# The gate and up blocks of a feed-forward network: four quads in blocks 3 to 10, and two pairs a block with their low parts from an adding DMA

## Chip, cores and metric

The kernel runs on one core of a Trainium2 chip. The metric is the device time of one execution in microseconds (us), given as the median of several runs. Engines are named as in the profile: PE (TensorE, matrix products), DVE (VectorE), ACT (ScalarE), POOL (GpSimd), SP (SyncE, which issues loads).

## What is computed

One layer on 256 tokens of width 2048, in fp32: a SwiGLU network, a mixer (an RWKV7 scan, a pooling branch and an output projection) and a second SwiGLU network, each between two RMS norms and added to the residual. The change lies in the two SwiGLU networks:

```python
def _swiglu(x, w_gate, w_up, w_down):          # x: 256 x 2048, D_FF = 5632
    return (jax.nn.silu(x @ w_gate) * (x @ w_up)) @ w_down
...
    h = x
    f = _swiglu(_rmsnorm(h, ln_ffn1_pre[l]), ffn1_gate[l], ffn1_up[l], ffn1_down[l])
    h = h + MACARON_WEIGHT * _rmsnorm(f, ln_ffn1_post[l])
    mx = _hybrid_mixer(_rmsnorm(h, ln_mix_pre[l]), ...)
    h = h + _rmsnorm(mx, ln_mix_post[l])
    f = _swiglu(_rmsnorm(h, ln_ffn2_pre[l]), ffn2_gate[l], ffn2_up[l], ffn2_down[l])
    h = h + MACARON_WEIGHT * _rmsnorm(f, ln_ffn2_post[l])
```

## The kernel before

**Products.** PE multiplies in fp32r, a shorter form of fp32. So every operand is kept as a high part (rounded to fp32r) and a low part (what is left), and a product is three matmuls: high by high, low by high, high by low (`mm3`, L316 to L320). One matmul is 128 x 128 by 128 x 512. For every weight tile ACT makes the high part (a cast) and DVE the low part (the weight less the high part).

**Blocks.** The gate and up weights of a network are cut into 11 blocks of 512 columns (0 to 10). In a block the 2048 rows are 16 k-tiles of 128. A *pair* is two k-tiles of one weight for both token halves: one load of 128 x 1024, a cast (L372), a low (L382) and 12 matmuls (`fetch` L361, `pair` L538). A *quad* (`quad` L549) takes two k-tiles of gate and up together in a Strassen-like scheme: 7 products instead of 8, so 21 matmuls stand for the 24 of a gate pair and an up pair. It costs DVE three sums of weights (t13 at L570, t2 at L575, t4 at L579) and four lows (L592), and ACT four casts (L587). `seven` (L502) runs a block: after its last quad `merge` (L642, additions at L639) adds the quads' products up, then come Silu (L1061), the product of gate and up (L1068) and a transpose (L869). The carry (`carry`) moves the result with 16 small DMAs of POOL (L886) to the layout that the down product wants; ACT and DVE split it at L899 and L903.

**The order of a block** stands in a string of `GATE_UP` (L48): f is the next gate pair, l the next up pair, q the next quad. Quads take the first k-tiles, pairs the others. Block 1 is sixteen pairs; the others alternate:

```python
GATE_UP = ["", "ffffffffllllllll"] + ["fffqffqllqlll", "ffqfqfqlqlll"] * 4 + ["fffqffqllqlll"]
```

So blocks 2, 4, 6, 8, 10 have three quads and five gate and five up pairs (183 matmuls), blocks 3, 5, 7, 9 have four quads and four of each (180 matmuls). A capital F or L is a pair whose low part a DMA adds; no string has one.

**Buffers and order.** Weights land in w32 (4 buffers) or in general units of 128 x 1024; 33 units exist, and activations and the tiles of h hold more and more of them as blocks go by. High and low parts go to a ring of 5 (wH, wL), or to units (kH, kL). A planner (`Plan.solve`, L136) fixes the order on each engine from rough costs before the kernel is written: it follows the PE order, gives each step a due time, starts loads at most `FETCH` (22 us) ahead of it, and takes buffers as they come free. Loads are issued by SP, in order; SP waits until the target buffer is free, and what stands behind waits too. ACT, DVE and POOL also work their queues in order.

Of the kernel before, what the change touches and what calls it, by code (L numbers as in the profile page):

```python
# [23 lines left out]
W = 1024  # L24
# [22 lines left out]
OUT = ((0, "", 0), (1, "fffqfq" "qlqlll", 0), (3, "", TRAIL))  # L47
GATE_UP = ["", "ffffffffllllllll"] + ["fffqffqllqlll", "ffqfqfqlqlll"] * 4 + ["fffqffqllqlll"]  # L48
SUMS = (2, 2)
# [7 lines left out]
EARLY = 0.5  # L57
RATE, LEAVE, LAND, ADD, MOVE = 0.28, 1.05, 2.0, 10.0, 12.0

# [29 lines left out]
class Plan:  # L89
# [46 lines left out]
    def solve(s):  # L136
# [46 lines left out]
        while len(order) < len(s.nodes):  # L183
# [17 lines left out]
            if n.size:  # L201
                start = max(n.free + LEAVE, line)
                line = start + n.size / RATE
                n.end = max(n.end, (line if n.eng == "SP" else n.free + LEAVE + n.size / RATE)
                            + LAND)
            for k in n.rel:
# [13 lines left out]
class Block:  # L220
# [140 lines left out]
    def fetch(s, w, k, c0, keep, hold=False, by_dma=False):  # L361
# [29 lines left out]
        return p.op("DVE", cost("DVE", 1024), low, [n], rel=[src]), dst  # L391

    def halves_of(s, w32, hold=False):
        if hold:
            wH, wL = s.unit(dt=F32R, p="kH"), s.unit(dt=F32R, p="kL")
        else:
            wH = s.wp.tile([P, 1024], F32R, tag="wH", name=s.nm("wH"), bufs=WS_BUFS)
            wL = s.wp.tile([P, 1024], F32R, tag="wL", name=s.nm("wL"), bufs=WS_BUFS)
        return [t.rearrange("p (k c) -> p k c", k=2) for t in (w32, wH, wL)]
# [102 lines left out]
    def seven(s, wf, cf, wl, cl, at, dep, KT, need, sm, order, ev_f, ev_l, used, trail=0):  # L502
# [27 lines left out]
        def rows(k, h):  # L530
            xH, xL = at(k)
            return xH[:, h * P:h * P + P], xL[:, h * P:h * P + P]
# [5 lines left out]
        def pair(k, w, c0, b, by_dma):  # L538
            low, dst = s.fetch(w, k, c0, keep, by_dma, by_dma)

            def do():
                for i in range(2):
                    for h in range(2):
                        mul(f"{b}{h}", rows(k + i, h), ws[k + i])
            d = p.pe(12 * MM, do, [low, dep(k)] + claim(b + "0", b + "1"), dst)
            used.setdefault(k // 4, []).append(d)
            return d
# [105 lines left out]
        nq, last = 0, {}  # L653
        ks = dict(f=iter(range(K0, KT, 2)), l=iter(range(K0, KT - trail, 2)))
        for c in order:
# [9 lines left out]
            w_ = (wf, cf) if c == "f" else (wl, cl)  # L665
            last[c] = pair(next(ks[c]), *w_, c, by_dma)
            left[c] = left.get(c, 0) + 1
# [1338 lines left out]
```

## Time and profile before

| | |
|---|---|
| runs shown | 3: median 2019.09 us (2018.82 to 2020.29) |
| profiled execution | 2018.42 us, span of its instructions 2016.7 us |
| granted PE clock | 0.999 |
| busy in the span | PE 99%, DVE 90%, ACT 59%, POOL 16% |
| loads (queue q1) | 384.70 MB in 204649 packets |
| matmuls of 128 x 512 in the six largest groups | 3 x 2128 for pairs, 3 x 270 for quads |

A view by stretch gives each engine's busy time between two times. A view by group gives busy time, count and mean of one, and the idle time just before with what ended it. The timeline gives instructions by start. A busy PE means that matmuls are in flight, not that it runs at its peak.

### The profile page before, as it was taken

What the parts mean: (1) busy time and instruction counts of PE and PEld (TensorE: products, weight loads), DVE (VectorE), ACT (ScalarE), POOL (GpSimd) and SP (SyncE); (2) the same over time, 40 slices, a digit from 0 to 9 for tenths busy, and PEclk for the clock granted to TensorE, in tenths of its full rate; (3) what the DMA queues carried; (4) which work ended last, traced back from release to release, by engine and by line L of the source; (5) the groups of instructions that cost most, each with busy time, mean ns of one, the idle gap of its engine ahead of it and who ended that gap; (6) DMA issues with size and microseconds to landing.
All of it is one profiled execution on the core that took longest, in us unless ns stands there. A gap on an engine that the chain in (4) does not pass through costs nothing.

```text
span 2016.7 us, 28695 instructions
## 1 busy us (share of the span) xinstructions
PE 2002.8 (99%) x9963; PEld 1655.3 (82%) x9963; DVE 1821.7 (90%) x2418; ACT 1189.3 (59%) x1582; POOL 326.3 (16%) x673
## 2 busy tenths in 40 slices
PE   9999999999999999999999999999999999999997
PEld 7888888888888888888788788888888888888886
DVE  6999999999999957799689678979999999999997
ACT  7565665656666566685476435665566556556663
POOL 0111131131000123413220111011121211310000
PEclk9999999999999999999999999999999999999999
DMA  7775565676568677757456558667656656765683
GB/s 270 254 239 173 188 217 200 203 221 228 186 203 299 209 212 213 205 175 214 147 173 189 159 168 269 245 218 245 223 176 202 218 196 190 230 229 188 207 294 126
DMA packets 227355, 423.56 MB, mean 210 GB/s; under 512 B 24575, under 2 KB 28041, under 8 KB 227209
## 3 DMA queue, kind: packets, MB, share of 16 engines
q1 hardware_dynamic: 204649, 384.70, 59.2%
q0 software_dynamic: 22272, 36.51, 5.5%
q8 instruction: 78, 1.28, 0.3%
q10 hardware_dynamic: 288, 0.52, 0.1%
q14 instruction: 68, 0.56, 0.1%
HBM read 396.69 MB, written 8.39 MB: 201 GB/s over the span
## 4 chain that ended last, share of the span: by engine, by line
PE 97%; DVE 1%; issue 1%; DMA 0%; ACT 0%; POOLq 0%; POOL 0%; DVEq 0%; SPq 0%
PE mm L318 27%; PE mm L320 26%; PE mm L319 26%; PE ms L319 5%; PE ms L320 5%; PE ms L318 5%; PE tr L843 1%; PE pA L1724 0%; DVE u L639 0%; PE mc L811 0%; PE pU L1820 0%; PE pSa L1832 0%; DMA w<-in_ffn_gate_dram 0%; PE pY L1855 0%; PE pT L1891 0%
## 5 line engine op out<-in xcount | busy, mean ns | idle before, releaser
L318 PE MATMUL mm<-wH,xH 128*128 128x512 f32 (+1 forms) x2128 | 830.1, 391 | 0.0
L320 PE MATMUL mm<-wH,xL 128*128 128x512 f32 (+1 forms) x2128 | 825.8, 388 | 0.5 <-DVE xL L861 0.5
L319 PE MATMUL mm<-wL,xH 128*128 128x512 f32 (+1 forms) x2128 | 825.7, 388 | 0.0
L320 PEld LDWEIGHTS mm<-wH,xL 128*128 128x128 f32 x2128 | 399.4, 188 | 83.5 <-DVE xL L861 1.4
L318 PEld LDWEIGHTS mm<-wH,xH 128*128 128x128 f32 x2128 | 399.5, 188 | 82.5 <-ACT xH L852 0.2
L319 PEld LDWEIGHTS mm<-wL,xH 128*128 128x128 f32 x2128 | 399.7, 188 | 80.6
L372 ACT CAST wH<-w 128x1024 fp32r<-128x1024 f32 x317 | 330.7, 1054 | 224.8 <-PE mm L320 192.2
L382 DVE TENSOR_TENSOR wL<-w,wH 128x1024 fp32r<-128x1024 f32 x317 | 377.9, 1217 | 22.8 <-ACT wH L372 20.4
L587 ACT CAST wH<-t 128x1024 fp32r<-128x1024 f32 x204 | 215.1, 1055 | 226.2 <-PE mm L320 117.7
L295 DVE TENSOR_TENSOR wL<-w,wH 128x1024 fp32r<-128x1024 f32 (+2 forms) x200 | 236.5, 1191 | 94.9 <-ACT wH L294 93.3
L294 ACT CAST wH<-w 128x1024 fp32r<-128x1024 f32 (+2 forms) x200 | 205.3, 1034 | 171.0 <-PE mm L320 149.7
L886 POOL DMA_DIRECT2D x<-T x352 | 172.5, 497 | 730.5 <-DVE T L869 245.5
L592 DVE TENSOR_TENSOR wL<-t,wH 128x1024 fp32r<-128x1024 f32 x204 | 242.8, 1215 | 1.7 <-ACT wH L587 1.7
L587 ACT CAST wH<-w 128x1024 fp32r<-128x1024 f32 x204 | 165.6, 834 | 50.4 <-PE mm L320 30.8
L592 DVE TENSOR_TENSOR wL<-w,wH 128x1024 fp32r<-128x1024 f32 x204 | 191.2, 950 | 0.0
L570 DVE TENSOR_TENSOR t<-w,w 128x1024 f32<-128x1024 f32 x102 | 123.9, 1215 | 0.0
L319 PE MATMUL ms<-wL,sH 128*128 128x512 f32 x270 | 105.5, 391 | 0.2
L320 PE MATMUL ms<-wH,sL 128*128 128x512 f32 x270 | 105.1, 389 | 0.0
L318 PE MATMUL ms<-wH,sH 128*128 128x512 f32 x270 | 105.1, 389 | 0.0
L579 DVE TENSOR_TENSOR t<-w,t 128x512 f32<-128x512 f32 x102 | 70.3, 689 | 2.2
L575 DVE TENSOR_TENSOR t<-w,t 128x512 f32<-128x512 f32 x102 | 69.9, 686 | 1.1
L639 DVE TENSOR_TENSOR u<-ms,u 128x512 f32<-128x512 f32 x92 | 61.3, 685 | 1.4
(313 smaller groups left out, 2099.3 us busy)
## 6 DMA issues: line engine op xcount, KB each, us to landing
w<-in_w_in_dram SPq DMA_DIRECT2D x128, 512.0 KB
w<-in_ffn_up_dram SPq DMA_DIRECT2D x114, 512.0 KB
w<-in_ffn_gate_dram SPq DMA_DIRECT2D x112, 512.0 KB
w<-in_ffn_down_dram SPq DMA_DIRECT2D x104, 512.0 KB
w<-in_ffn_down_dram SPq DMA_DIRECT2D x144, 256.0 KB
w<-in_ffn_gate_dram SPq DMA_DIRECT2D x128, 256.0 KB
w<-in_ffn_up_dram SPq DMA_DIRECT2D x124, 256.0 KB
w<-in_w_out_dram SPq DMA_DIRECT2D x24, 512.0 KB
```

What stands on the lines that cost most here:

```text
L294: s.nc.scalar.copy(vH, v)
L295: s.nc.vector.tensor_tensor(out=vL, in0=v, in1=vH.bitcast(F32), op=ALU.subtract)
L318: nc.tensor.matmul(ps, aH, bH, start=start, stop=False)
L319: nc.tensor.matmul(ps, aH, bL, start=False, stop=False)
L320: nc.tensor.matmul(ps, aL, bH, start=False, stop=stop)
L372: nc.scalar.copy(x["H"], x["v"])
L382: nc.vector.tensor_tensor(out=x["L"], in0=x["v"], in1=x["H"].bitcast(F32), op=ALU.subtract)
L570: V.tensor_tensor(out=v["t13"], in0=v["a"], in1=v["b"][:, :1].to_broadcast([P, 2, 512]), op=ALU.subtract)
L579: V.tensor_tensor(out=v["t24"][:, 1], in0=v["b"][:, 1], in1=v["t24"][:, 0], op=ALU.subtract)
L587: nc.scalar.copy(H, src)
L592: V.tensor_tensor(out=L, in0=src, in1=H.bitcast(F32), op=ALU.subtract)
L886: nc.gpsimd.dma_start(out=x[0][q * 32:q * 32 + 32, i], in_=src[i * 32:i * 32 + 32, q])
```

## The change

Blocks 3 to 10 all get the string `ffqfqFqlqllL`: four quads, four gate pairs and four up pairs, 180 matmuls. Block 2 keeps three quads. The third gate pair (F) and the last up pair (L) are always k-tiles 14 and 15 (`KM`), and take a new way, `fetch_added`: the weight is loaded into a unit, ACT casts the high part (L404), ACT also writes the negated weight in fp32r (L408), and a DMA issued by POOL adds the weight to it, unit to unit in SBUF (L411). DVE has no part in it. Such a pair holds three units; the weight's is free when the add has landed. Its load stands outside the chain that orders the others and may start 28 us ahead (`FETCH + AHEAD`). The planner's time for an add goes from 10 to 8, and a DMA of POOL now counts in the line of transfers as those of SP do.

```diff
--- before.py
+++ after.py
@@ -45,7 +45,7 @@
 DOWN = ((0, "fffffffffffqfff" "qllqllqllqllqllqllqll", 0),
         (2, "fqflqfqflqfqflqfqflqfqfqff", TRAIL))
 OUT = ((0, "", 0), (1, "fffqfq" "qlqlll", 0), (3, "", TRAIL))
-GATE_UP = ["", "ffffffffllllllll"] + ["fffqffqllqlll", "ffqfqfqlqlll"] * 4 + ["fffqffqllqlll"]
+GATE_UP = ["", "ffffffffllllllll"] + ["fffqffqllqlll", "ffqfqFqlqllL", "ffqfqFqlqllL", "ffqfqFqlqllL", "ffqfqFqlqllL", "ffqfqFqlqllL", "ffqfqFqlqllL", "ffqfqFqlqllL", "ffqfqFqlqllL"]
 SUMS = (2, 2)
 BY_DMA = range(0)
 LAT = dict(PE=0.22, DVE=0.1, ACT=0.17, SP=0.0, POOL=8.0)
@@ -55,7 +55,8 @@
 SPARE, KEEP, URGENT, HOLD = 3, 4, 8.0, 99
 SOON, FETCH, LATEST, BEFORE = 22.0, 22.0, 12.0, 12.0
 EARLY = 0.5
-RATE, LEAVE, LAND, ADD, MOVE = 0.28, 1.05, 2.0, 10.0, 12.0
+AHEAD, MSPARE, KM = 6.0, 0, 14
+RATE, LEAVE, LAND, ADD, MOVE = 0.28, 1.05, 2.0, 8.0, 12.0
 
 ROWS = [("ln_mix_pre", 16), ("ln_ffn2_pre", 16), ("mu", 26), ("w0", 8), ("a0", 8),
         ("k_k", 8), ("k_a", 8)]
@@ -201,8 +202,7 @@
             if n.size:
                 start = max(n.free + LEAVE, line)
                 line = start + n.size / RATE
-                n.end = max(n.end, (line if n.eng == "SP" else n.free + LEAVE + n.size / RATE)
-                            + LAND)
+                n.end = max(n.end, line + LAND)
             for k in n.rel:
                 k.left -= 1
                 k.end = max(k.end, n.end)
@@ -390,6 +390,31 @@
             return p.op("POOL", 1.25, low, [n], size=0.94, lat=ADD), dst
         return p.op("DVE", cost("DVE", 1024), low, [n], rel=[src]), dst
 
+    def fetch_added(s, w, k, c0, keep):
+
+        nc, p, x = s.nc, s.plan, {}
+        dst = [Tok("unit"), Tok("unit"), Tok("unit")]
+        by_k = lambda t: t.rearrange("p (k c) -> p k c", k=2)
+
+        def load():
+            x["W"] = s.get_w(w, k, 2, c0, 512, own=dst[0].of == "unit")
+
+        def cast():
+            x["H"] = s.unit(dt=F32R, p="kH")
+            nc.scalar.copy(x["H"], x["W"])
+
+        def minus():
+            x["L"] = s.unit(dt=F32R, p="kL")
+            nc.scalar.activation(out=x["L"], in_=x["W"], func=AF.Copy, scale=-1.0)
+
+        def low():
+            nc.gpsimd.dma_start(out=x["L"], in_=x["W"], accum_op=ALU.add)
+            keep([(k + i, by_k(x["H"])[:, i], by_k(x["L"])[:, i]) for i in range(2)])
+        n = p.op("SP", 0.4, load, take=dst[:1], size=0.52, ahead=FETCH + AHEAD, spare=MSPARE)
+        h = p.op("ACT", cost("ACT", 1024), cast, [n], take=dst[1:2])
+        n = p.op("ACT", cost("ACT", 1024), minus, [n, h], take=dst[2:])
+        return p.op("POOL", 1.25, low, [n], size=0.94, lat=ADD, rel=dst[:1]), dst[1:]
+
     def halves_of(s, w32, hold=False):
         if hold:
             wH, wL = s.unit(dt=F32R, p="kH"), s.unit(dt=F32R, p="kL")
@@ -536,12 +561,14 @@
             ws.update((k, (wH, wL)) for k, wH, wL in tiles)
 
         def pair(k, w, c0, b, by_dma):
-            low, dst = s.fetch(w, k, c0, keep, by_dma, by_dma)
+            got = {}
+            low, dst = (s.fetch_added if by_dma else s.fetch)(
+                w, k, c0, lambda tiles: got.update((i, wt) for i, *wt in tiles))
 
             def do():
                 for i in range(2):
                     for h in range(2):
-                        mul(f"{b}{h}", rows(k + i, h), ws[k + i])
+                        mul(f"{b}{h}", rows(k + i, h), got[k + i])
             d = p.pe(12 * MM, do, [low, dep(k)] + claim(b + "0", b + "1"), dst)
             used.setdefault(k // 4, []).append(d)
             return d
@@ -651,7 +678,8 @@
                 held[b].append(d)
                 use[i][1].append(d)
         nq, last = 0, {}
-        ks = dict(f=iter(range(K0, KT, 2)), l=iter(range(K0, KT - trail, 2)))
+        ks = {c: iter([k for k in range(K0, k1, 2) if k != KM or c.upper() not in order])
+              for c, k1 in (("f", KT), ("l", KT - trail))}
         for c in order:
             if c == "q":
                 last["q"] = quad(nq)
@@ -663,7 +691,7 @@
                 continue
             by_dma, c = c in "FL", c.lower()
             w_ = (wf, cf) if c == "f" else (wl, cl)
-            last[c] = pair(next(ks[c]), *w_, c, by_dma)
+            last[c] = pair(KM if by_dma else next(ks[c]), *w_, c, by_dma)
             left[c] = left.get(c, 0) + 1
             if c == "f" and left["f"] == std // 2:
                 m["f"] = last["f"]
```

The lines below L205 move by up to 28: L570, L575, L579, L587 and L592 become L597, L602, L606, L614 and L619, L886 becomes L914, L899 becomes L927; L372 and L382 stay.

DVE, first network, block 4, around its second and third quads: t13 and t24 are sums of weights of one quad, wL from w32 at L382 is a pair's low, wL at L592 or L619 a quad's. Before:

```order
L570 TENSOR_TENSOR t13_523_2306<-w32_494_2166,w32_497_2177 128x1024
L575 TENSOR_TENSOR t24_526_2311<-w32_494_2166,t13_523_2306 128x512
L382 TENSOR_TENSOR wL_525_2309<-w32_478_2087,wH_524_2308 128x1024
L592 TENSOR_TENSOR wL_529_2318<-w32_481_2106,wH_528_2317 128x1024
L592 TENSOR_TENSOR wL_533_2330<-w32_482_2109,wH_532_2329 128x512
L579 TENSOR_TENSOR t24_526_2311<-w32_497_2177,t24_526_2311 128x512
L592 TENSOR_TENSOR wL_538_2344<-t13_513_2254,wH_537_2343 128x1024
L592 TENSOR_TENSOR wL_540_2361<-t24_521_2295,wH_539_2360 128x1024
L570 TENSOR_TENSOR t13_541_2371<-w32_509_2244,w32_510_2247 128x1024
L575 TENSOR_TENSOR t24_544_2376<-w32_509_2244,t13_541_2371 128x512
L382 TENSOR_TENSOR wL_543_2374<-w32_489_2146,wH_542_2373 128x1024
```

and now:

```order
L597 TENSOR_TENSOR t13_527_2312<-w32_502_2186,w32_503_2188 128x1024
L619 TENSOR_TENSOR wL_526_2310<-t24_519_2268,wH_525_2309 128x1024
L602 TENSOR_TENSOR t24_529_2322<-w32_502_2186,t13_527_2312 128x512
L606 TENSOR_TENSOR t24_529_2322<-w32_503_2188,t24_529_2322 128x512
L597 TENSOR_TENSOR t13_533_2330<-w32_507_2214,w32_509_2218 128x1024
L382 TENSOR_TENSOR wL_532_2328<-w32_501_2184,wH_531_2327 128x1024
L619 TENSOR_TENSOR wL_538_2345<-w32_502_2186,wH_537_2344 128x1024
L619 TENSOR_TENSOR wL_540_2349<-w32_503_2188,wH_539_2348 128x512
L602 TENSOR_TENSOR t24_547_2381<-w32_507_2214,t13_533_2330 128x512
L619 TENSOR_TENSOR wL_546_2365<-t13_527_2312,wH_545_2364 128x1024
L619 TENSOR_TENSOR wL_549_2384<-t24_529_2322,wH_548_2383 128x1024
L606 TENSOR_TENSOR t24_547_2381<-w32_509_2218,t24_547_2381 128x512
```

Where each quad had a pair's low behind it, two quads' sums now stand together with one pair's low.

ACT, the same block: wH is a tile of the ring, xH a tile of h, kH and kL are a pair's high part and negated weight in units. Before:

```order
L587 CAST wH_457_1982<-w32_410_1767 128x512
L587 CAST wH_459_1998<-t13_433_1893 128x1024
L587 CAST wH_463_2019<-t24_437_1912 128x1024
L899 CAST xH_465_2024<-x32_401_1734 128x4x128 x2
L372 CAST wH_469_2043<-w32_418_1818 128x1024
L372 CAST wH_471_2055<-w32_424_1842 128x1024
L587 CAST wH_473_2065<-w32_427_1865 128x1024
```

and now:

```order
L1089 ACTIVATE u_427_1854<-u_427_1854 128x512
L614 CAST wH_429_1875<-t13_413_1788 128x1024
L404 CAST kH_436_1905<-w32_423_1834 128x1024
L408 ACTIVATE kL_438_1910<-w32_423_1834 128x1024
L614 CAST wH_440_1926<-t24_432_1881 128x1024
L372 CAST wH_444_1940<-w32_398_1706 128x1024
L614 CAST wH_448_1950<-w32_404_1748 128x1024
```

The cast at L404 and the negated copy at L408 stand in a row among the ring's casts; kL_438 is the low part of block 4's up pair, which PE uses 130 matmuls after it first uses wH_440, the cast behind it.

POOL, first network, blocks 0 to 4: x32<-T1 are the carry's moves, kL<-w32 the adds. Before:

```order
L886 DMA x32_198_786<-T1_192_761 32x256 x16
L886 DMA x32_297_1270<-T1_294_1251 32x256 x16
L886 DMA x32_401_1734<-T1_391_1684 32x256 x16
L886 DMA x32_468_2030<-T1_462_2004 32x256 x16
L886 DMA x32_571_2497<-T1_559_2441 32x256 x16
```

and now:

```order
L914 DMA x32_198_786<-T1_192_761 32x256 x16
L914 DMA x32_298_1272<-T1_294_1251 32x256 x12
L411 DMA kL_311_1332<-w32_293_1249 128x1024
L914 DMA x32_298_1272<-T1_294_1251 32x256 x4
L411 DMA kL_352_1524<-w32_333_1443 128x1024
L411 DMA kL_392_1681<-w32_378_1624 128x1024
L914 DMA x32_401_1719<-T1_395_1695 32x256 x16
L411 DMA kL_438_1910<-w32_423_1834 128x1024
L411 DMA kL_478_2065<-w32_465_2010 128x1024
```

The adds stand between the moves of one block's carry and the next, the first of them inside one.

## The prediction

> **What bounds the kernel now.** I read the page first: busy times, then the chain that ended last.
>
> ```profile
> span 2016.7 us, 28695 instructions
> PE 2002.8 (99%) x9963; PEld 1655.3 (82%) x9963; DVE 1821.7 (90%) x2418; ACT 1189.3 (59%) x1582; POOL 326.3 (16%) x673
> PE 97%; DVE 1%; issue 1%; DMA 0%; ACT 0%; POOLq 0%; POOL 0%; DVEq 0%; SPq 0%
> ```
>
> PE is busy for 99% of the span and carries 97% of the chain. A busy PE need not be at its peak, so I looked next at the changed place alone: busy time by stretch, one stretch for each gate/up block. Counting 192 + 192 + 183 matmuls for blocks 0 to 2 puts block 3 of the first FFN at 140.34 us. Columns: length, then busy time and count of each engine, granted clock, DMA share, GB/s.
>
> ```profile
> core 0: us, PE busy (x) PEld busy (x) DVE busy (x) ACT busy (x) POOL busy (x), PEclk, DMA share, GB/s
> 140.34:181.14 40.80, 40.80 (x182) 33.78 (x180) 40.56 (x47) 25.23 (x28) 7.82 (x16) 1.00 0.68 230
> 181.14:222.62 41.48, 41.48 (x185) 34.35 (x183) 41.27 (x50) 24.73 (x29) 7.81 (x16) 1.00 0.60 198
> 387.25:428.20 40.95, 40.95 (x182) 33.70 (x180) 40.71 (x48) 23.93 (x26) 7.82 (x16) 1.00 0.69 210
> 428.20:469.68 41.48, 41.48 (x185) 34.35 (x183) 40.83 (x47) 24.36 (x27) 7.83 (x16) 1.00 0.74 229
> 140.34:469.68 329.34, 329.34 (x1454) 272.43 (x1452) 326.26 (x374) 196.62 (x220) 62.62 (x128) 1.00 0.64 208
> 1448.78:1778.10 329.32, 329.32 (x1453) 272.44 (x1452) 326.23 (x374) 196.58 (x220) 62.61 (x128) 1.00 0.64 208
> ```
>
> The first row is block 3 (four quads), the second block 4 (three quads). 40.80 us for 180 weight loads, one for each matmul, and 41.48 us for 183 are both 0.2267 us for one matmul, at full clock. 1452 x 0.2267 is 329.1, so in blocks 3 to 10 PE loses about 0.2 us an FFN. PE is the limit and its work is what must shrink. But DVE stands right behind: 326.26 of 329.34 us, idle 0.24 and 0.21 us in the first two rows. Both engines have to be followed.
>
> **PE's part of the change.** A quad is 21 matmuls in place of the 24 of a gate pair and an up pair. Blocks 4, 6, 8 and 10 go from three quads to four, in both FFNs: 8 quads, 24 matmuls less, which is also the difference between the two PE orders. 24 x 0.2267 = **5.44 us less**. As PE is never idle there, this is a gain in full if nothing else comes late. More is hardly possible: the waits left to remove are 2 x 0.2 us.
>
> **DVE's part.** A stretch of DVE's timeline, with one quad and one pair (start, length):
>
> ```profile
> 310.75 1.22 DVE L570 TENSOR_TENSOR t<-w,w 128x1024 f32<-128x1024 f32 x1
> 312.00 0.69 DVE L575 TENSOR_TENSOR t<-w,t 128x512 f32<-128x512 f32 x1
> 312.61 1.22 DVE L382 TENSOR_TENSOR wL<-w,wH 128x1024 fp32r<-128x1024 f32 x1
> 313.74 1.22 DVE L592 TENSOR_TENSOR wL<-w,wH 128x1024 fp32r<-128x1024 f32 x1
> 314.88 0.69 DVE L579 TENSOR_TENSOR t<-w,t 128x512 f32<-128x512 f32 x1
> 315.48 0.68 DVE L592 TENSOR_TENSOR wL<-w,wH 128x512 fp32r<-128x512 f32 x1
> 316.08 2.36 DVE L592 TENSOR_TENSOR wL<-t,wH 128x1024 fp32r<-128x1024 f32 x2
> 318.36 1.22 DVE L570 TENSOR_TENSOR t<-w,w 128x1024 f32<-128x1024 f32 x1
> ```
>
> Instructions overlap a little, so I take starts: the pair's low costs 313.74 - 312.61 = 1.13 us, the quad (318.36 - 310.75) - 1.13 = 6.48 us. A block that gains a quad loses two pairs to it and gives two more lows to the DMA: 6.48 - 4 x 1.13 = +1.96 us. A block that had four quads gives two lows away: -2.26 us. Over blocks 3 to 10: 4 x (1.96 - 2.26) = -1.2 us an FFN, while PE loses 2.72. DVE idles 329.34 - 326.26 = 3.08 us now, of which eight times some 0.21 (rows above) lies between dependent steps; 1.4 us is spare. It needs 1.5. So DVE ends level with PE, at most 0.1 us over in an FFN. What improves is the spread: by the same numbers a four-quad block now asks DVE for some 2 us more than PE and a three-quad block gives it back; afterwards every block is even.
>
> **The adding DMA.** The trace of before has none, so I bound it. Rows: DMA issues (count, size, median us to landing), POOL's time for one issue, the landing of the gain rows, and the load queue:
>
> ```profile
> x<-T POOLq DMA_DIRECT2D x352, 32.0 KB, 5.0
> h<-hsp POOLq DMA_DIRECT2D x8, 512.0 KB, 7.0
> xr<-in_x_dram POOLq DMA_DIRECT2D x4, 512.0 KB, 9.3
> L1146 POOL DMA_DIRECT2D gb<-in_ln_ffn_post_dram x4: 543/559/568, 640.9 to 1959.0; - x4
> DMA to landing us min/median/max: 5.6/6.8/9.1
> L886 POOL DMA_DIRECT2D x<-T x352 | 172.5, 497 | 730.5 <-DVE T L869 245.5
> q1 hardware_dynamic: 204649, 384.70, 59.2%
> ```
>
> From below it lands after 5.0 us (a move within SBUF, 1/16 of the size). From above, as it reads its target too, I take twice the slowest plain one: 18.6 us. I take 9, nearest to the 512 KB rows. It has more: in the new orders 103 to 136 matmuls stand between the first use of the tile that ACT casts right after the negated copy and the first use of that pair's low, 23 to 31 us. So its own landing is hidden, and POOL pays some 0.55 us an issue, with 62.6 of 329 us busy. Behind an add on POOL wait the carry's moves, whose tiles are wanted first by ACT's casts at L899 and then by the down product.
>
> The Trainium skill, "DMA: Bandwidth & Descriptors" (Anatomy of one DMA, SWDGE path), fits 2.0 us plus bytes over 436 GB/s. That would be an estimate of 3.2 us for one pass of 512 KB; this trace does not agree, its 512 KB rows say 5.6 to 9.3 us, and the measurement decides.
>
> On the DMA engines: 384.70 MB took 59.2% of the span, so 512 KB takes 1.6 us of all sixteen; one add is 1.6 to 3.3 us, two a block are 8 to 16 points on a share of 0.60 to 0.74. There is room on the mean, not at each moment. In the last blocks ACT already waits for loads (first stretch: blocks 8 to 10; total, times, longest):
>
> ```profile
> ACT wH L372 <- DMA w<-in_ffn_gate_dram: 2.1, 2, 1.2
> ACT wH L372 <- DMA w<-in_ffn_down_dram: 1.6, 2, 1.3
> ACT wH L587 <- DMA w<-in_ffn_gate_dram: 1.1, 2, 0.7
> ```
>
> Such a wait of up to 1.3 us costs PE nothing (block 10 takes 41.48 like block 4). The same skill page (Issuing engines are not separate DMA queues) speaks against the change here: DMAs from any engine run on the same sixteen and interleave. Queue q0 beside q1 can't show more in this trace; by that rule an add lengthens a load that meets it, which is the second case below.
>
> **ACT, SP and the planner.** A cast of a pair:
>
> ```profile
> L372 ACT CAST wH<-w 128x1024 fp32r<-128x1024 f32 x317 | 330.7, 1054 | 224.8 <-PE mm L320 192.2
> ```
>
> ACT gets 24 instructions more an FFN (a quad has four casts, a pair one, the negated copy is new): at most 25 us at 1.05 on 196.62 of 329. Free, unless its queue stands still: behind the cast at L404 wait the ring's casts. SP issues two loads more for each new quad, and the third gate and last up load move out of their chain, 28 us ahead. These pairs hold three units, W until the add has landed. Only at some places does SP wait for a landed add: there the next such pair's load takes that W. I cost this at nothing in the likeliest case, as 9 us fit; both ends stand in the fourth case. The queue of POOL transfers, now counted into the planner's landing times, reorders the loads of gains and residuals alone; nothing on the path.
>
> **Sum.** The profiled execution took 2018.42 us (span 2016.7 and 1.7 around it): 2018.42 - 5.44 + 0.2 = 2013.2. The median, 2019.09, stands 0.67 above it: some **2013.8 us**.
>
> **The cases.** (1) *As summed*: 0.58, 2013.8, between 2013.2 (none of the 0.2, PE's old waits gone) and 2014.9.
>
> (2) *Loads come late in blocks 8 to 10*: six adds there an FFN, twelve in all. For it: the waits above, 0.74 in block 10. Against: ACT hides 1.3 us, the load bytes are the same. If a third of the twelve meet a load that is just due, 4 x (1.6 to 3.3 less 1.3) is 1 to 8 us; I take 3.5: 2017.3. Chance 0.20.
>
> (3) *DVE runs out of lead at the start of a block*: the merge of the block before and the first quad now stand together. In block 8, between a pair's low and the next one, DVE has some 16 us of work (6 instructions of 1024 columns at 1.13 and 15 of 512 at 0.6, by the starts above) while PE needs it after 33 matmuls, 7.5 us: it must enter 8.4 us ahead. For it: DVE is full. Against: the last up pair isn't in the ring, so the ring's five tiles reach 54 matmuls ahead, 12.2 us less a cast and a low of 2.3. A lead short by 0.25 us in sixteen blocks costs 4: 2017.8. Chance 0.10.
>
> (4) *The add lands too late for the next load* (slower): from one such pair's cast to the next lie about 84 matmuls, 19.0 us. Cast, copy and issue take 2.6, the next load up to 5.6 (the fastest row of its size): beyond some 11 us of landing, ACT stands still at three hand-overs an FFN. At 15 us: (15 - 11 - 1.3) x 6 = 16 us lost: 2030. Against: no 512 KB row is over 9.3. Chance 0.10.
>
> (5) *It does not do what it says*: the orders show 24 matmuls less and 32 adds, so 0.02, at 2019.1.
>
> **Chances and range.** 0.2% (4 us) is about what a measurement of this kernel can tell from no change. Faster by more means under 2015.05: case 1, a third of case 2 and a little of 3: 0.66. Slower by more, over 2023.1: most of case 4, 0.09. Within: 0.25. The range runs from 2012.8 (case 1 with the runs' scatter of 0.3 below the median) to 2018.2, so that it holds cases 1 and 3 and most of 2, and leaves out 4.
>
> **What the profile after would show.** Right: blocks 3 to 10 are 326.4 us long in each FFN, 40.80 each, PE busy throughout; DVE at some 325 us with a gap under 0.3 in each block; adds landing in 6 to 11 us. Wrong in case 2: PE idle behind DVE lows whose casts waited for loads, in blocks 8 to 10 alone. In case 3: PE idle at each block's start with ACT and loads early. In case 4: SP waiting for the add, ACT's L404 cast waiting for its load. The prediction falls if landing is over 11 us, or if the rest of the span, outside the sixteen blocks, moves by more than 0.5 us.

## The result and the profile after

The changed kernel takes **2023.01 us** (median of 14 runs, 2021.43 to 2025.55) beside 2018.95 us before (14 runs, 2018.60 to 2020.29): ratio 1.0020, 95% interval 1.0012 to 1.0028. It is slower by 0.2%, where 2013.8 was forecast, and it lies outside the range. The profiled execution took 2024.09 us.

The page after, with the same three lines as before:

```profile
span 2022.4 us, 28830 instructions
PE 1999.5 (99%) x9939; PEld 1649.8 (82%) x9939; DVE 1817.7 (90%) x2426; ACT 1228.9 (61%) x1630; POOL 356.3 (18%) x705
PE 78%; DVE 13%; DMA 4%; issue 4%; ACT 1%; SPq 0%; DVEq 0%; POOLq 0%; POOL 0%; ACTq 0%
```

PE has 24 matmuls less and is busy for less time, yet the span grew by 5.7 us; and the chain that ended last, 97% PE before, runs for 13% through DVE and for 4% through DMAs. Busy shares hardly moved. The chain says where to look.

Busy time by stretch after: block 7, 8, 9 and 10 and blocks 3 to 10 of the first FFN, then block 6 and blocks 3 to 10 of the second:

```profile
303.98:344.78 40.80, 40.80 (x182) 33.79 (x180) 39.32 (x47) 25.29 (x29) 9.71 (x18) 1.00 0.77 235
344.78:386.48 41.70, 41.09 (x182) 33.71 (x180) 39.55 (x46) 26.10 (x29) 9.66 (x18) 1.00 0.82 241
386.48:428.02 41.54, 41.09 (x182) 33.71 (x180) 40.99 (x48) 27.03 (x30) 9.71 (x18) 1.00 0.77 228
428.02:468.82 40.80, 40.80 (x182) 33.80 (x180) 40.59 (x50) 27.85 (x34) 8.77 (x17) 1.00 0.66 203
140.78:468.82 328.04, 326.99 (x1442) 270.19 (x1440) 321.25 (x372) 213.84 (x239) 76.65 (x143) 1.00 0.76 230
1571.48:1613.81 42.33, 41.09 (x182) 33.71 (x180) 39.20 (x45) 26.43 (x30) 11.05 (x21) 1.00 0.72 220
1449.08:1779.80 330.72, 327.64 (x1442) 269.97 (x1441) 321.28 (x371) 213.72 (x239) 76.56 (x143) 1.00 0.75 228
```

Read length against 40.80 first: some blocks are exactly what was forecast, others lose 0.7 to 1.7 us. Then DVE: in block 7 it idles 1.5 us while PE loses nothing (its lead pays), in blocks 8 and 9 the lead is gone. Last the DMA share: 0.76 and 0.75 over blocks 3 to 10, 0.64 before. The loads are the same 384.70 MB in all, so the rise of 0.12 x 328 us over 16 adds gives an estimate of 2.4 us of all sixteen DMA engines for one add.

Waits after (total, times, longest): DVE's in blocks 3 to 10 of the first FFN, then DVE's and ACT's largest for loads in those of the second:

```profile
DVE wL L382 <- ACT wH L372: 3.5, 4, 1.8
DVE t L597 <- DMA kL<-w: 1.2, 1, 1.2
...
DVE wL L382 <- ACT wH L372: 4.4, 6, 1.5
DVE t L597 <- DMA kL<-w: 2.9, 1, 2.9
ACT wH L372 <- DMA w<-in_ffn_up_dram: 4.3, 3, 1.9
ACT wH L614 <- DMA w<-in_ffn_gate_dram: 3.6, 3, 2.2
ACT kH L404 <- DMA w<-in_ffn_up_dram: 3.4, 4, 2.5
```

DVE waits 4.7 and 7.3 us; before it was this one row, alike in both FFNs:

```profile
DVE wL L382 <- ACT wH L372: 0.9, 2, 0.6
```

One of these waits in the timeline of the second FFN (DVE, POOL, PE; the bracket is the idle time before and what ended it):

```profile
1598.06 2.35 DVE L619 TENSOR_TENSOR wL<-t,wH 128x1024 fp32r<-128x1024 f32 x2
1603.33 1.23 DVE L597 TENSOR_TENSOR t<-w,w 128x1024 f32<-128x1024 f32 x1 [2.92 <-DMA kL<-w]
1604.47 3.49 DVE L382 TENSOR_TENSOR wL<-w,wH 128x1024 fp32r<-128x1024 f32 x3
...
1594.45 0.86 POOL L411 DMA_DIRECT2D kL<-w  x1 [15.85 <-ACT kL L408]
...
1605.74 0.50 PE L319 MATMUL mm<-wL,xH 128*128 128x512 f32 x1 [1.24 <-DVE wL L382]
```

The add is issued at 1594.45 and has landed some 8.8 us later. The next quad's t13 (now L597) writes into the unit that held the added pair's weights, so DVE stands still for 2.9 us with three lows behind it, and PE then waits for the first of them. The first matmul that uses the added low itself comes at 1631.72, 28 us after the landing.

By stretches between counted matmuls, after less before: blocks 3 to 10 -1.30 and +1.40 us (forecast -2.9 each), the two down phases +1.16 and +1.37, from the last matmul to the end +2.62, the first 140 us +0.44 (they differ by up to 3.8 us from run to run), all else within 0.01 us.

The end is one instruction that the views leave out and the trace records: a closing DRAIN of POOL, on which the end of the program waits.

```
              start      length   span ends
before      2007.36     8.57 us     2016.72
after       2010.42    11.18 us     2022.39
```

### The profile page after: what moved, and what is told of

Its sections match the earlier page's. It is cut to its first block, busy times and chain, and to the rows that moved or that the text cites. A ratio compares the mean times of both kernels' runs of the same rounds, so it can differ in the third digit from the quotient of the medians.

```text
span 2022.4 us, 28830 instructions
## 1 busy us (share of the span) xinstructions
PE 1999.5 (99%) x9939; PEld 1649.8 (82%) x9939; DVE 1817.7 (90%) x2426; ACT 1228.9 (61%) x1630; POOL 356.3 (18%) x705
## 3 DMA queue, kind: packets, MB, share of 16 engines
q1 hardware_dynamic: 204905, 384.70, 57.6%
## 4 chain that ended last, share of the span: by engine, by line
PE 78%; DVE 13%; DMA 4%; issue 4%; ACT 1%; SPq 0%; DVEq 0%; POOLq 0%; POOL 0%; ACTq 0%
PE mm L318 22%; PE mm L319 21%; PE mm L320 21%; PE ms L319 3%; DVE wL L619 3%; PE ms L320 3%; PE ms L318 3%; DVE wL L382 2%; DMA w<-in_ffn_gate_dram 2%; DVE u L666 2%; DMA w<-in_ffn_down_dram 2%; DVE t L597 1%; DVE t L602 1%; DVE t L606 1%; PE tr L871 1%
## 5 line engine op out<-in xcount | busy, mean ns | idle before, releaser
L319 PE MATMUL mm<-wL,xH 128*128 128x512 f32 (+1 forms) x1952 | 758.0, 388 | 4.0 <-DVE wL L382 3.9
L318 PE MATMUL mm<-wH,xH 128*128 128x512 f32 (+1 forms) x1952 | 761.3, 391 | 0.2 <-ACT xH L880 0.2
L320 PE MATMUL mm<-wH,xL 128*128 128x512 f32 (+1 forms) x1952 | 757.5, 388 | 0.5 <-DVE xL L889 0.4
L319 PEld LDWEIGHTS mm<-wL,xH 128*128 128x128 f32 x1952 | 366.6, 188 | 80.2 <-DVE wL L382 7.0
L320 PEld LDWEIGHTS mm<-wH,xL 128*128 128x128 f32 x1952 | 366.4, 188 | 76.5 <-DVE xL L889 1.3
L318 PEld LDWEIGHTS mm<-wH,xH 128*128 128x128 f32 x1952 | 366.3, 188 | 76.1 <-ACT xH L880 0.5
L372 ACT CAST wH<-w 128x1024 fp32r<-128x1024 f32 x269 | 280.1, 1053 | 165.0 <-PE mm L320 126.8
L614 ACT CAST wH<-t 128x1024 fp32r<-128x1024 f32 x220 | 231.6, 1054 | 192.9 <-DVE t L606 66.4
L382 DVE TENSOR_TENSOR wL<-w,wH 128x1024 fp32r<-128x1024 f32 x269 | 322.2, 1218 | 26.3 <-ACT wH L372 25.5
L619 DVE TENSOR_TENSOR wL<-t,wH 128x1024 fp32r<-128x1024 f32 x220 | 262.3, 1216 | 0.0
L614 ACT CAST wH<-w 128x1024 fp32r<-128x1024 f32 x220 | 178.3, 836 | 95.0 <-PE mm L320 61.2
L914 POOL DMA_DIRECT2D x<-T x352 | 174.5, 510 | 347.6 <-DVE T L897 127.9
L619 DVE TENSOR_TENSOR wL<-w,wH 128x1024 fp32r<-128x1024 f32 x220 | 205.8, 950 | 0.0
L597 DVE TENSOR_TENSOR t<-w,w 128x1024 f32<-128x1024 f32 x110 | 133.7, 1215 | 4.1 <-DMA kL<-w 4.1
L411 POOL DMA_DIRECT2D kL<-w x32 | 28.7, 896 | 361.0 <-ACT kL L408 251.7
L606 DVE TENSOR_TENSOR t<-w,t 128x512 f32<-128x512 f32 x110 | 75.9, 690 | 2.8
L602 DVE TENSOR_TENSOR t<-w,t 128x512 f32<-128x512 f32 x110 | 75.4, 686 | 1.2
```

The lines of the kernel that those rows point to most:

```text
L318: nc.tensor.matmul(ps, aH, bH, start=start, stop=False)
L319: nc.tensor.matmul(ps, aH, bL, start=False, stop=False)
L320: nc.tensor.matmul(ps, aL, bH, start=False, stop=stop)
L372: nc.scalar.copy(x["H"], x["v"])
L382: nc.vector.tensor_tensor(out=x["L"], in0=x["v"], in1=x["H"].bitcast(F32), op=ALU.subtract)
L597: V.tensor_tensor(out=v["t13"], in0=v["a"], in1=v["b"][:, :1].to_broadcast([P, 2, 512]), op=ALU.subtract)
```

## The experiments

Theories: **1, lead**: DVE is level with PE and without the short blocks runs out of lead. **2, transfers**: the adds make DVE wait, (2a) by their bytes, which make loads late, or (2b) by holding units until they land. **3**: POOL's closing DRAIN grows with its DMAs. The table has for each run its median, and the length against the kernel before (profiled executions) of blocks 3 to 10 and the down phase of each FFN, and of the end. "Loss" is the sum of the four beyond that of e5, which has the same matmuls and no transfer. Each run stood beside runs of the kernel before, whose median was 2018.60 to 2018.98 us, and each ratio is against those.

| run | median us | blocks 3-10 | down | blocks 3-10 | down | end | loss |
|---|---|---|---|---|---|---|---|
| after | 2023.01 | -1.30 | +1.16 | +1.40 | +1.37 | +2.62 | 8.3 |
| e1 last block three quads | 2028.24 | +1.00 | +1.76 | +0.72 | +1.63 | +2.61 | |
| e2 adds only | 2024.76 | +0.04 | 0.00 | -0.20 | +0.03 | +2.61 | |
| e3 quads only | 2039.40 | +7.57 | +2.74 | +7.54 | +2.81 | 0.00 | 26.4 |
| e4 before, 32 DMAs of POOL | 2022.00 | -0.05 | 0.00 | +0.25 | +0.02 | +2.62 | |
| e5 no add | 2013.07 | -2.94 | +0.05 | -2.92 | +0.10 | 0.00 | 0 |
| e6 1/16 of the bytes | 2015.95 | -2.94 | 0.00 | -2.92 | +0.09 | +2.61 | 0 |
| e7 before, 80 DMAs of POOL | 2017.68 | -0.01 | +0.01 | +0.23 | +0.06 | -1.71 | |
| e8 planner's add 10 us | 2025.70 | +0.42 | +1.25 | +0.62 | +1.49 | +2.61 | 9.5 |
| e9 tile added to itself | 2020.79 | -2.35 | +1.73 | -1.57 | +1.15 | +2.61 | 4.7 |
| e10 after, 48 DMAs of POOL | 2018.49 | -1.14 | +1.51 | -0.69 | +1.61 | -1.91 | 7.0 |
| e11 8 adds an FFN | 2015.85 | -0.92 | 0.00 | -0.89 | +0.02 | -1.85 | |
| e12 12 adds, 3 quads | 2018.51 | -1.43 | +1.02 | -0.85 | +0.94 | -1.65 | |
| e13 plain copy | 2016.66 | -2.94 | +0.03 | -2.92 | +0.31 | +2.61 | 0.2 |
| e14 10 adds, 2 quads | 2015.84 | -0.88 | +0.48 | -1.56 | +0.05 | -1.87 | |
| e15 12 adds, 2 quads | 2017.49 | -1.58 | +1.32 | -1.54 | +1.35 | -1.88 | |

### e3 and e2: one half of the change alone

```diff
-GATE_UP: "ffqfqFqlqllL" in blocks 3 to 10
+e3: "ffqfqfqlqlll" in blocks 3 to 10 (no adds)
+e2: "ffqfqFqlqllL", "fffqfFqllqllL" by turns (four and three quads as before, two adds in each)
```

> The changed kernel's quad counts (four in each of blocks 3 to 10), with every low made by DVE: the quads without the adds. PE has 24 matmuls less than before, as in the changed kernel. DVE gains 4 x (6.48 - 2 x 1.13) = 16.9 us an FFN, 343.2 us of work against PE's 326.6. Theory 1: DVE sets the length, some 344 us for blocks 3 to 10 less the lead of 5 to 8 us that it can use up: +8 to +15 us an FFN, +16 to +30 us in all against before. Rival (DVE's work is not what stalls PE; the adds are): 326.6 us for the eight blocks, 5.4 us faster than before. Theory 3: without adds the final drain is back to 8.6 us (11.2 in the changed kernel).

Ratio 1.0103 (1.0088 to 1.0119), as the first theory had it. DVE sets the length, +20.7 us in gate/up and down, and the end is as before. Without the adds the quads cannot be paid for: that part of the reasoning stands.

> The kernel before with its quad counts (4, 3, 4, 3 ... 3), but the third gate pair and the last up pair of blocks 3 to 10 get their low from the adding DMA: the adds without the new quads. PE's work is as before, DVE loses 2 x 1.13 us in every block, 18 us an FFN. Theory 1 (lost lead of DVE): with that much slack on DVE no PE stall is left in blocks 3 to 10 and in the down phases, 329.2 us for the eight blocks. Theory 2 (the adds stall the path themselves, by landing late for the unit that the next quad's DVE step takes, and by late loads): DVE still waits for the landing of adds, and if this alone is what stalls PE, some 1 to 3 us an FFN are lost. Theory 3 (the final drain of GpSimd grows with the number of its DMAs): the end of the span is 2.6 us later than before, total time +2.6 to +3 us against before; if the growth at the end comes from the new quads or from jitter, 0.

Ratio 1.0028 (1.0017 to 1.0038). Blocks 3 to 10 of the first FFN, then DVE's and ACT's largest waits there:

```profile
140.54:469.92 329.38, 329.38 (x1453) 272.49 (x1452) 308.00 (x354) 208.20 (x234) 76.88 (x143) 1.00 0.76 229
```

```profile
DVE wL L382 <- ACT wH L372: 13.9, 14, 2.6
DVE wL L619 <- ACT wH L614: 3.9, 4, 2.1
ACT wH L372 <- DMA w<-in_ffn_gate_dram: 6.4, 5, 2.7
```

DVE waits for 18 us and PE loses nothing: with 21 us to spare the waits are free. So the adds do no harm as such; they do it to a DVE that has no slack. Of the 5.8 us by which the median is up, 2.6 are the end, and 3.65 us lie in the mixer, where DVE and ACT run some instructions in another order than in the kernel before. This belongs to neither half; e1 has it too.

### e1: three quads in the last block

```diff
-block 10: "ffqfqFqlqllL"
+block 10: "fffqfFqllqllL"
```

> The changed kernel, but block 10, the last gate/up block of each FFN, keeps three quads (with the two adds in it, so DVE loses two lows there). PE gets 2 x 3 matmuls back, +1.36 us against the changed kernel. Theory 1 (lead: DVE enters the down phase with less in hand, because the last block no longer gives any back): the PE stalls in the two down phases (0.82 and 0.99 us after, none before) go to under 0.3 us in all, and the down phases are as long as before; blocks 3 to 9 keep their stalls. Time about equal to the changed kernel's, -0.3 to +0.3 us. Rival (adds and loads crowd the DMA engines, and the down phase starts with late loads): the stalls of the down phases stay, time +1.4 us. Both leave the end of the span (final drain 11.2 us) as in the changed kernel.

The time was missed: ratio 1.0047 (1.0034 to 1.0059), 5.2 us above the changed kernel, with 3.65 of the mixer's order and 1.36 of matmuls in it. The down phases seem to lose more instead of less, +1.76 and +1.63, but not at the same place. In the changed kernel their loss lies in their first 70 us (all but 0.05 us of it); in e1 the first 182 us lose only 0.26 and 0.29, and the rest stands in the last 45 us. The largest stall there, at 687.99, waits for a pair's low (kL, L382) that DVE makes only at 686.72, behind additions of the quads' products (L666): the planner put them in that order here. So the stalls that theory 1 spoke of do go, and others come from a new order.

### e5, e6, e13, e9: what of the transfer costs

All four keep the changed kernel's order on every engine and alter one line.

```diff
-nc.gpsimd.dma_start(out=x["L"], in_=x["W"], accum_op=ALU.add)
+e5:  pass
+e6:  nc.gpsimd.dma_start(out=x["L"][:, :64], in_=x["W"][:, :64], accum_op=ALU.add)
+e13: nc.gpsimd.dma_start(out=x["L"], in_=x["L"])
+e9:  nc.gpsimd.dma_start(out=x["L"], in_=x["L"], accum_op=ALU.add)
```

> The changed kernel with the same order on every engine, but the adding DMA itself is not issued: the low of these 32 pairs stays the negated copy, so that part of the product is not computed. It takes away the transfers, what waits for their landing, and GpSimd's 0.9 us for each; the loads, casts, copies and the new quads stay. DVE waits 4.7 and 7.3 us in blocks 3 to 10 of the two FFNs after the change and 0.9 us before; PE loses 1.4 + 1.2 and 4.1 + 1.4 us in gate/up and down. Theory 2 (the transfers make the waits: a unit of the memory is handed on only when the add has landed, and the loads share the DMA engines with them): DVE's waits fall to about 1 to 2 us an FFN and PE's loss to under 2 us in all; with the final drain back at 8.6 us the time is about 2014.5. Rival (the new order makes the waits: loads that are issued late and two more loads for each new quad): DVE still waits 3 us or more an FFN, PE still loses 5 to 8 us, and only the drain's 2.6 us is gained: about 2020.

> The changed kernel with the same order, but each adding DMA moves 64 of the 1024 columns (1/16 of the bytes): the rest of the low stays the negated copy, so part of the product is not computed. The number of DMAs, GpSimd's issues and the waits for landings stay; the traffic of 16.8 MB goes. If the traffic on the DMA engines makes the loads late: PE's loss of 8.1 us falls to under 3, time about 2018 (the drain stays at 11.2 us). If the landing itself counts (its latency, and where the plan hands the unit on): landing stays near 4.5 us, DVE's two waits for it shrink but the rest stays, time 2020 to 2023.

e5: ratio 0.9971 (0.9959 to 0.9982). e6: 0.9988 (0.9979 to 0.9996). Blocks 3 to 10 of both FFNs in e5, of the first in e6:

```profile
141.20:467.60 326.40, 326.40 (x1441) 270.27 (x1440) 322.39 (x373) 215.28 (x241) 62.62 (x128) 1.00 0.64 207
1446.71:1773.11 326.40, 326.40 (x1442) 270.27 (x1440) 322.40 (x373) 215.30 (x241) 62.58 (x128) 1.00 0.64 207
```

```profile
144.16:470.56 326.40, 326.40 (x1441) 270.36 (x1440) 322.39 (x373) 215.32 (x241) 76.66 (x143) 1.00 0.66 208
```

PE is busy throughout, to the 326.40 us of the forecast, and DVE's wait is one row of 1.6 us in each. So the rival of e5, the new order, is out: the loads, casts, copies, issues and the order cost PE nothing, and the transfers in their full size cost all. e6 takes away the bytes but also shortens the landing (median 3.5 us instead of 6.2), so two more runs part them:

> The changed kernel with the same order; each adding DMA keeps its size but adds the tile of the low to itself instead of adding the loaded weights, so its bytes stay on the DMA engines while the loaded weights' unit no longer waits for its landing (it is free when ScalarE has made the negated copy). The low of these pairs is wrong, so part of the product is not computed. Without the transfer, and with 1/16 of it, PE lost nothing in blocks 3 to 10 (326.40 us each). Theory 2a (the bytes: they make the loads late that share the DMA engines): PE's loss stays, 6 to 8 us in all, time 2021 to 2023. Theory 2b (the hand-over: DVE stands behind the landing of an add whose unit its next step takes): PE's loss falls to 0 to 2 us, time 2015 to 2017. Where both count, DVE's waits for a landing (1.2 and 2.9 us) go and those for late casts (3.5 and 4.4 us) stay: about 2019.

> As the run in which the low's tile is added to itself, but as a plain copy of that tile onto itself: the same 512 KB, order, issues and count, without accumulation (the low stays the negated copy, so part of the product is not computed). With accumulation PE lost 4.8 us against the run without transfers, time 2020.8; with 1/16 of the bytes none, 2016.0. If any 512 KB transfer makes the loads late: about 2020 to 2021. If it is the accumulation, whose target is read and written as well: 2016 to 2017.5.

Blocks 3 to 10 of both FFNs, of e9 and then of e13:

```profile
141.22:468.21 326.99, 326.92 (x1441) 270.21 (x1440) 320.92 (x371) 213.01 (x239) 76.72 (x143) 1.00 0.77 231
1448.99:1776.74 327.75, 326.95 (x1441) 270.19 (x1440) 321.49 (x372) 213.75 (x239) 76.59 (x143) 1.00 0.77 230
```

```profile
140.44:466.84 326.40, 326.40 (x1441) 270.27 (x1440) 322.38 (x373) 214.91 (x241) 71.52 (x143) 1.00 0.71 231
1446.00:1772.40 326.40, 326.40 (x1442) 270.27 (x1441) 322.12 (x373) 215.19 (x241) 71.35 (x143) 1.00 0.71 231
```

DVE's waits in the second FFN, of e5 (all it has), of e9 (which has 0.2 us more for a load) and of e13:

```profile
DVE wL L382 <- ACT wH L372: 1.6, 3, 1.2
```

```profile
DVE wL L382 <- ACT wH L372: 3.9, 6, 1.2
```

```profile
DVE wL L382 <- ACT wH L372: 2.0, 4, 1.2
```

The transfers themselves (ns of POOL for one issue, then us to the landing, each min, median, max), e9 then e13:

```profile
L411 POOL DMA_DIRECT2D kL<-kL x32: 859/902/934, 125.9 to 1738.6; - x32
DMA to landing us min/median/max: 4.5/6.7/9.2
```

```profile
L411 POOL DMA_DIRECT2D kL<-kL x32: 530/551/571, 124.9 to 1733.5; - x32
DMA to landing us min/median/max: 2.9/4.8/7.0
```

e9: ratio 1.0008 (0.9999 to 1.0017), between its two theories: DVE no longer waits for a landing, but 3.8 and 3.9 us for late casts (as after the change), and 4.7 of the 8.3 us are still lost. e13: 0.9989 (0.9980 to 0.9998), nothing lost in blocks 3 to 10, as its second theory had it. The same 16.8 MB on the same queue at the same places, once added and once copied: the **accumulation** makes the difference. It raises the DMA share from e5's 0.64 by 0.13 instead of 0.07, which over 327 us and 16 transfers gives an estimate of 2.7 us of all sixteen engines for one instead of 1.4, and POOL needs 0.90 us for its issue instead of 0.55. The plain copy makes loads late too, but ACT hides it: ACT's waits for loads in the two stretches are 4.6 and 4.6 us in e5, 7.5 and 8.6 in e13, 12.6 and 10.8 in e9, and only in e9 do DVE's waits grow by more than 0.4. The hand-over (2b) is the rest: 2.2 us by the medians, 2.3 to 3.6 by the losses (of e10 and of after, which have one order). The intervals of e9 and of the changed kernel overlap, so its amount is less sure than that it occurs, which the timeline shows.

PE, DVE, ACT and SP have one order in blocks 3 to 10 and the down phases of after, e5, e6, e9, e10 and e13, so DVE's waits can be set against PE's loss. For each FFN: how much longer DVE waits in blocks 3 to 10 than in e5, and what PE loses there and in the down phase behind, both beyond e5:

| run | waits, 1st | loss, 1st | waits, 2nd | loss, 2nd |
|---|---|---|---|---|
| after | 3.1 | 2.8 | 5.7 | 5.6 |
| e10 | 3.1 | 3.3 | 4.0 | 3.7 |
| e9 | 2.2 | 2.3 | 2.5 | 2.4 |
| e13 | 0.0 | 0.0 | 0.4 | 0.2 |
| e6 | 0.0 | 0.0 | 0.0 | 0.0 |

To within 0.4 us, what DVE waits beyond e5's 1.6 us is what PE loses. What gate/up doesn't show of it comes in the down phase: at the end of block 10 DVE's instructions start later against PE's than in e5 by 1.1 and 1.25 us in the changed kernel and by 1.6 and 1.1 in e9, and the down phases lose 1.1 and 1.3, and 1.7 and 1.05 more than e5's.

### e8: the planner told 10 us

```diff
-RATE, LEAVE, LAND, ADD, MOVE = 0.28, 1.05, 2.0, 8.0, 12.0
+RATE, LEAVE, LAND, ADD, MOVE = 0.28, 1.05, 2.0, 10.0, 12.0
```

> The changed kernel, but the planner counts 10 us instead of 8 from GpSimd's issue to the landing of an add, as the constant was before; so it hands the unit of an added pair on later, and every engine's order in the gate/up blocks is planned anew. If it is the hand-over of a unit on a landing that was planned too early that makes DVE wait (1.2 and 2.9 us, the rest of the queue behind): those waits vanish, PE loses 3 to 4 us less, time about 2019 to 2020. If the waits come from loads that are late as such: DVE's waits move but do not shrink, time 2022 to 2025.

The first theory missed; the rival's sign came, at a time just above its range. Ratio 1.0034 (1.0022 to 1.0047). The group of t13 shows no wait for an add any more (after, it had 4.1 us of it), but others of the same size:

```profile
L597 DVE TENSOR_TENSOR t<-w,w 128x1024 f32<-128x1024 f32 x110 | 133.7, 1215 | 4.3 <-PE mm L319 2.6 <-DMA w<-in_ffn_gate_dram 1.6
```

Planning around the landing moves the waits (5.3 us in blocks 3 to 10 of each FFN) to another unit and to a late load; DVE's lack of slack stays.

### e4, e7, e10: the end of the span

```diff
+for i in range(32):
+    nc.gpsimd.dma_start(out=more[i], in_=prm["w_proj_a"][:P, :128])
```

This is e4. In e7 it is `range(80)`, and in e10, within the changed kernel, `range(48)`, both with `[:1, :128]`.

> The kernel before, with 32 plain DMAs more that GpSimd issues at the start of the mixer (64 KB each, DRAM to DRAM, 128 rows, read by nobody): extra work, the outputs are unchanged. It has as many more GpSimd DMAs as the change has adds, without accumulation and far from the end. Theory 3 (the final drain of GpSimd grows with the number of its DMAs or of their descriptors): the drain takes 11.2 us instead of 8.6, time +2.6 us plus what the issues cost in the mixer (32 x 0.55 us on GpSimd, which is not full there). Rival (only accumulating transfers, or transfers of that size, or the place late in the program make it longer): the drain stays at 8.6 us, time +0 to +1 us.

> The kernel before with 80 DMAs more from GpSimd at the start of the mixer, of one row of 512 bytes each (read by nobody; outputs unchanged). 32 more made the final drain 2.61 us longer, 82 ns for each, whatever their size, yet all 572 of the kernel before cost only 8.57 us, 15 ns each. Theory 3a (the drain is linear in the number, from some base): 80 x 82 ns = 6.5 us longer, 15.1 us, time +6.5 to +7. Theory 3b (the drain walks what has been used of a ring of 128, or another power of two, since it last came round: 572 is 60 over 4 x 128, 604 is 92 over): 652 is 12 over 5 x 128, so the drain takes some 8.57 - 48 x 0.082 = 4.6 us, time 4 us less than before.

> The changed kernel with 48 DMAs more from GpSimd at the start of the mixer, of one row of 512 bytes each (outputs unchanged): 652 in all, as many as the kernel before had with 80 more, where the final drain took 5.22 us. Theory 3b (the drain depends on the number modulo 128 alone, whoever issued them): 5.22 us instead of 11.18; the end of the span then waits for the last outputs, 1.71 us earlier than in the kernel before, so 2.62 + 1.71 = 4.3 us less than the changed kernel: 2018.7. Rival (the adds make the drain long in themselves): it stays at 11.2 us or grows, 2023 or more.

Ratios 1.0013 (1.0004 to 1.0022), 0.9995 (0.9985 to 1.0004), 1.0000 (0.9991 to 1.0008). e4 and e10 came as the number of DMAs had it; in e7 the DRAIN got shorter, as theory 3b had it, but the time fell by 0.9 us and not by 4. The closing DRAIN by the number of POOL's DMAs, as the traces record them (the expectations counted four fewer in each: 572, 604 and 652):

```
number      576     608     656
DRAIN us   8.57   11.18    5.22
runs    before,  after, e4,   e7, e10, e11,
         e3, e5  e1, e2, e6,  e12, e14, e15
                 e8, e9, e13
```

32 plain DMAs of 64 KB, which POOL issued in its first 28 us, gave to the hundredth what 32 adds of 512 KB gave: kind, size and place do not count, the number does. And it does not simply grow: at 656 it is shorter than at 576. A ring of 128 would fit (64, 96 and 16 past a multiple), though the step from 16 to 64 is 70 ns a DMA and that from 64 to 96 is 82; it is not shown, for no other numbers were tried. Filling the number up to 656 gives the changed kernel 4.5 us back by the medians; in the kernel before it is 1.7 us of the profiled end and about 1 us of the median, too little to tell from no change. At 656 the last outputs, and no longer the DRAIN, end the span (e7: the DRAIN ends at 2013.67 us, the last output lands at 2015.00).

### e11, e12, e14, e15: smaller doses

The number of POOL's DMAs is 656 in all four. The planner makes a new order for each, so two of them differ by more than their adds.

```diff
+blocks     3 4 5 6 7 8 9 10      (M: ffqfqFqlqllL, 4: four quads, 3: three, both without adds)
+e11        M M M M 4 3 4 3
+e14        M M M M M 3 4 3
+e15        M M M M M 3 M 3
+e12        M M M M M M 4 3
```

> A smaller dose, with outputs as the reference: of blocks 3 to 10, blocks 3 to 6 have four quads and two adds each, 7 and 9 four quads, 8 and 10 three quads without adds; 64 one-row DMAs from GpSimd bring their number to 652. Against the kernel before PE has 2 x 2 x 3 matmuls less, 2.7 us; DVE gets two quads and gives 8 lows away, 2 x (6.48 - 2.26) - 9.04 = -0.6 us an FFN. Half of the adds' bytes, and in the blocks with the lower DMA share. If lead and bytes are the whole story: no PE stall, and 2.7 + 1.7 us (the drain) less than the kernel before: 2014.4. If adds stall PE in any case, half the changed kernel's loss (4 us): 2018.4.

> As the run with two more quads and 8 adds an FFN, with two more adds in block 7 (10 an FFN; 60 one-row DMAs keep the number at 652); outputs as the reference. There blocks 9 took 41.46 us instead of 40.80 and nothing else was lost. If DVE lacked lead before block 9: 2 x 1.13 us more lead, block 9 takes 40.80, 1.3 us less in all: 2014.5. If the bytes of the adds count: PE stalls appear in blocks 7 to 9, 2015.9 or more.

> The same with two more adds in block 9 (12 an FFN, blocks 3 to 7 and 9; 56 one-row DMAs keep the number at 652); outputs as the reference. DVE has 2 x 4.22 - 12 x 1.13 = -5.1 us an FFN against PE's -1.36, so more slack than in the kernel before. If lead is what decides, no PE stall in spite of three quarters of the bytes: 2014.5. If the bytes decide, more is lost than with 8 adds: 2016 or more.

> Between the two: blocks 3 to 8 have four quads and two adds each, 9 four quads and 10 three, both without adds; 56 one-row DMAs from GpSimd bring their number to 652; outputs as the reference. PE has 18 matmuls less than before, 4.1 us; DVE 3 x 4.22 - 12 x 1.13 = -0.9 us an FFN. If the loss grows in proportion to the adds (8.1 us for 32): 4.1 gained, 6.1 lost, 1.7 from the drain: about 2019. If the last block with three quads gives DVE its lead back and the adds of blocks 9 and 10 were the ones that hurt: 2013.2 to 2015.

Ratios 0.9984 (0.9975 to 0.9993), 0.9983 (0.9975 to 0.9992), 0.9993 (0.9984 to 1.0002), 0.9998 (0.9989 to 1.0007), in the order of the expectations. e11 and e14 lie between the times of their two theories, e15 took the time of its second, and e12 that of its first. Block 9 of the first FFN in e11, then blocks 9 and 6 in e14:

```profile
387.34:428.80 41.46, 41.29 (x182) 33.63 (x180) 41.18 (x48) 24.73 (x27) 7.83 (x16) 1.00 0.66 209
```

```profile
387.00:427.80 40.80, 40.80 (x181) 33.78 (x180) 40.63 (x48) 24.67 (x27) 3.92 (x8) 1.00 0.61 197
263.22:304.72 41.50, 41.13 (x181) 33.71 (x180) 39.23 (x45) 26.67 (x30) 9.71 (x18) 1.00 0.72 221
```

With two more lows given away in block 7, block 9 is whole in both FFNs: that one was lead (theory 1). But block 6, where DVE now idles 2.3 us, loses 0.7 in the first FFN: there DVE's t13 waits 2.1 us for a load of gate weights, so that one is a late load; what made it late was not parted. With 12 adds and two quads more (e15) blocks 3 to 10 are whole in both FFNs, and so are the first 182 us of the down phases, although DVE waits 5.8 and 5.7 us in the blocks: its 319.6 us of work leave it room. The 1.3 us that each down phase of e15 loses stand in the last 45 us, where e1 lost its own: the order there, not the adds. So e15's time, which its second theory gave, did not come by way of the bytes. With 12 adds and three quads more (e12) the blocks lose 0.8 and 1.4 us and the down phases 1.0 and 0.9, in their first 70 us. e11 and e14, at 2015.8, beat both kernels, by 3.1 and 7.2 us; of e11's profiled stretches the blocks gain 1.8 us and the shorter end, which e7 has too, 1.9.

## Why the prediction was wrong

**PE's part was right.** 24 matmuls, 5.44 us, "a gain in full if nothing else comes late": e5 and e13 gain 5.9 us in the sixteen blocks (with the 0.2 us that PE lost in each FFN).

**DVE's part** was right as work, and better than forecast: in e5 DVE is busy for 322.4 of 326.4 us, where some 325 was forecast. Some of that is work that falls outside the stretch; over the whole kernel its busy time fell by 4.1 us, where 2 x 1.2 was forecast. The step that failed is what followed from it. "DVE ends level with PE" was taken as enough, and the sum has no term for longer waits of DVE: what the added pairs hold up was put at "nothing in the likeliest case, as 9 us fit". But a level engine can make up no wait. DVE's waits grew by 3.8 and 6.4 us (3.1 and 5.7 beyond e5's), and PE lost 2.8 and 5.6. With room on DVE (e2, e15) waits of the same size and more cost nothing. That blocks with three quads used to pay such waits back, which the text counted as "spread" that improves, is argued and not shown.

**The adding DMA.** The forecast landing, 9 us within 5.0 to 18.6, was on the safe side: 4.5/6.2/10.2 us, the median under the forecast and the shortest under the lower bound. (The slowest plain 512 KB transfer of the kernel before took 11.5 us; "no 512 KB row is over 9.3" compares medians.) The slack of the low was right too, "so its own landing is hidden". Wrong was who else waits for it: the text looked for SP at the next load and found it harmless (case 4); it was DVE, whose t13 takes the freed unit, 7.6 and 8.8 us after the issue. The threshold of 11 us was worked out for the wrong waiter. The share of the DMA engines, "1.6 to 3.3 us" for one add, held (2.7 by the estimate from e9); but the loads' lateness was priced as case 2, in blocks 8 to 10 alone, less 1.3 us that ACT would hide, 3.5 us at a chance of 0.20. In e9, which has it without the hand-over, it was 4.7 us: 1.9 in blocks 9 and 10, and 2.7 in the down phases, which case 2 left out. That transfers of all issuers share the engines (the Trainium skill, "DMA: Bandwidth & Descriptors", Issuing engines are not separate DMA queues) was weighed there. The traces agree: from e5 to e13 and e9 the DMA share rises from 0.64 to 0.71 and 0.77, and ACT's waits for loads rise with it.

**Case 3** named a place rightly: in block 8 PE did lose 0.77 us, at 355.97, at the pair behind the first quad. Not as a cause: the same order without transfers has no stall in any block (e5).

**POOL** paid 0.90 us for an issue, not 0.55, and nothing came of it (e6 pays it too and loses nothing). Moves of the carry stood behind adds for 16.4 us in all, but no wait of PE for the carry's tiles is on record.

**The end** was no term at all. The prediction named "the rest of the span, outside the sixteen blocks" as what must not move; it moved by 2.6 us at the end (e4) and 2.5 in the down phases.

So the sum that was measured, by medians: 2018.95, less 5.9 for PE and its old waits (e5, 2013.1), plus 2.9 for the end (e6, 2016.0; the DRAIN is 2.6 of it), 0.7 for plain bytes (e13, within scatter), 4.1 for accumulating (e9, 2020.8), 2.2 for the hand-over (2023.0). The runs of the kernel before that stood beside them differ by up to 0.4 us, so each term is only as good as that.

## What to carry to other kernels

When an engine beside the bottleneck goes level with it, ask where the next microsecond of waiting would be made up; if nowhere, every microsecond that it waits becomes time. For a DMA that frees a buffer, list who takes that buffer next on every engine, not only who reads the result. Price an accumulating DMA apart from a copy of its size.

## What the hardware showed that was not expected

An accumulating DMA of 512 KB within SBUF took 0.90 us of POOL and, by the estimate from the DMA shares, 2.7 us of all sixteen DMA engines (e9); a plain copy took 0.55 and 1.4 (e13). POOL's closing DRAIN took 5.2, 8.6 or 11.2 us by the number of its DMAs in the whole program (656, 576, 608), whatever they moved and when.
